# SBUF tiles moved to multiples of 1 or 2 KB, and the low part of q laid on all 128 rows, in a two-block hybrid kernel

## The chip, the cores and the metric

The kernel runs on one core of a Trainium2 chip. The metric is device microseconds of one execution. A core has a matrix engine (TensorE, PE in the profile; its weight loads are shown as PEld), VectorE (DVE), ScalarE (ACT), GpSimd (POOL) and a queue engine (SyncE, SP) that issues the DMAs here. SBUF is the on-chip memory from which TensorE reads: a matmul has a stationary operand, loaded beforehand, and a moving operand that is streamed through; the product is added up in PSUM.

## The reference

512 tokens of width 1024 pass through two blocks. The first has two layers, each with softmax attention (8 heads of 64, relative bias) beside a retention path (4 heads of 128), gated and projected out. The second is a conformer: four gated feed-forward networks of width 2816, one convolution of 31 taps and one stick-breaking attention of 16 heads. The part of the softmax attention that matters here:

```python
scores = jnp.einsum("bnqhd,bnkhd->bnhqk", qc, kb) * (dh ** -0.5)
...
scores = jnp.where(valid, scores + bias[None, None], NEG_INF)
p = jax.nn.softmax(scores, axis=-1)
out = jnp.einsum("bnhqk,bnkhd->bnqhd", p, vb)
```

and the last feed-forward and norm: `h = h + HALF_STEP * swiglu_ffn(...)`, then `rms_norm_2(h, final_norm)`.

## The kernel before, in words

All activations stand transposed: 8 tiles `x` of 128 channels by 512 tokens. Every float32 operand of a large product is split into a rounded high part and the low rest (`split`, `scale_split`, `prepare` and `flush` for the weights), and `mm3` (L252 to L257) makes a product of three matmuls: high by high (L255), high weight by low activation (L256), low weight by high activation (L257). The weights come from HBM in pairs of blocks (`raw`), ACT rounds them (`wh`, L210) and DVE forms the rest (`wl`, L217) one or two blocks ahead of use. The order of the work on each engine is the order in which the program is written.

All large tiles come from one pool, `sb`, under tags: `x`, `raw`, `wh`, `wl`, `u` (32 buffers of 2 KB for each partition), `xg` (16 of 2 KB, the split activations that a projection streams) and `b` (8 of 5 KB, attention matrices and, as high and low halves of one tile, the hidden activations of a feed-forward, L871). In the pool a tag's buffers lie one after the other, behind the tags used before it. The constants lie ahead of the pool, and the small columns (`small`, L128) are a tag of the pool too; the first of them are made after `wl` and before the first `b`. In the built program `x`, `raw`, `u`, `xg`, `wh` and `wl` start 32 bytes past a multiple of 1 KB, and `b` 160 bytes past a multiple of 1 KB.

The softmax attention of a layer (in `hybrid`, L596) goes by four pairs of heads. For a pair `part("w_in", p)` projects q, then k is projected (L729 to L734, with the transposes of the pair before, `flip`, in between), then the gate. `q_out` (L680) scales q and lays out its two heads: `hi` holds the high part of a head on both halves of the 128 rows, `lo` the low part of both heads, each on its own 64 rows. `k_out` (L691) puts a head's high part on its own 64 rows and its low part on the other 64. `scores` (L701) makes, for each of four blocks of 128 queries, two matmuls into one place: L708 over 128 rows (high q by high and low k) and L709 over 64 rows (low q by high k). `softmax1` and `softmax2` follow on DVE and ACT while TensorE projects for the next pair.

Constants that only the set-up and a few later steps read: `cs` (L351, identity, triangle and a stripe of diagonals), `ident` (L357, read by `flip` L570 and `to_rows` L316), the stripe (L954, read by `diagonals` in the convolution).

Of the kernel before, what the change touches and what calls it, by code (L numbers as in the profile page):

```python
# [8 lines left out]
F32 = mybir.dt.float32  # L9
F32R = mybir.dt.float32r  # L10
I32 = mybir.dt.int32
AF = mybir.ActivationFunctionType
ALU = mybir.AluOpType

P = 128
# [17 lines left out]
CLIP = 256  # L33
EPS = 1e-6
LN_EPS = 1e-5
OFF = {512: 0, 384: 512, 128: 896, 256: 1024}


# [56 lines left out]
class Kernel:  # L95
    def __init__(self, ctx, tc, w, x, pos, vec, cst, relb, dec, out):
        self.tc = tc
        self.nc = tc.nc
        self.win, self.xin, self.pos, self.vecin, self.cst, self.relb, self.dec, self.out = (
            w, x, pos, vec, cst, relb, dec, out)  # L100
        self.pc = ctx.enter_context(tc.tile_pool(name="const", bufs=1))
        self.sb = ctx.enter_context(tc.tile_pool(name="sb", bufs=1))
        self.ps = ctx.enter_context(tc.tile_pool(name="ps", bufs=2, space=bass.MemoryType.PSUM))
        self.psb = None
        self.dr = ctx.enter_context(tc.tile_pool(name="dram", bufs=2, space=bass.MemoryType.DRAM))
        self.n = 0
        self.order = weight_order()
        self.chunks = []
        seen = {}
        for i in range(0, len(self.order), 2):  # L110
            k = self.order[i][3]
            assert self.order[i + 1][3] == k
            self.chunks.append((k, seen.get(k, 0)))
            seen[k] = seen.get(k, 0) + 1
        self.loaded = self.ready = self.used = 0
        self.raw = {}
        self.split_w = {}
        self.pending = []
# [8 lines left out]

    def small(self, cols):  # L128
        self.n += 1
        return self.sb.tile([P, cols], F32, name=f"s{self.n}", tag=f"small{cols}", bufs=4)  # L130

    def const(self, shape, dtype=F32):
        self.n += 1
# [210 lines left out]
    def setup(self):  # L344
        nc = self.nc
        nc.scalar.preload_act_table(AF.Sin)
        self.vec = self.const([P, NVEC])
        self.x = [self.tile("x") for _ in range(KT)]
        self.load_pieces()
        self.load()  # L350
        cs = self.const([P, 3, P])  # L351
        nc.sync.dma_start(cs, self.cst)
        nc.sync.dma_start(self.vec[:, 16:NVEC], self.vecin[:, 16:NVEC])
        self.posi = self.tile("u", I32)
        nc.sync.dma_start(self.posi, self.pos.partition_broadcast(P))
        self.cs = cs
        self.ident = cs[:, 0]  # L357
        self.ones2 = self.const([P, 2])
        nc.vector.memset(self.ones2, 1.0)
        self.mean = self.const([P, P])  # L360
        nc.gpsimd.memset(self.mean, 1.0 / D)
        self.mhalf = self.const([P, 4])
        nc.vector.memset(self.mhalf, -0.5)
        self.identr = self.const([P, P], F32R)
        self.tri = self.const([P, P], F32R)
        self.ones = self.const([P, P], F32R)
        self.rest = self.const([P, P], F32R)
        self.nmask = self.const([P, P], F32R)
        self.halfpi = self.const([P, 1])
        nc.vector.memset(self.halfpi, math.pi / 2)  # L370
        self.fgg = self.const([P, KT])
        self.hbias = self.const([P, 16])
        self.acc = None
        self.xg = []
        for m in range(KT):
            self.xg.append(self.scale_split(self.x[m], self.col("norm_gain", m)))
            if m == 2:
                self.acc = self.square_add(self.acc, self.x[0], 0)
            self.prepare_pieces(m)
        for m in range(1, SQ):  # L380
            self.acc = self.square_add(self.acc, self.x[m], m)

    def setup2(self):
        nc = self.nc
        cs = self.cs
        nc.vector.tensor_copy(out=self.identr, in_=cs[:, 0])
        nc.vector.tensor_scalar(self.tri, cs[:, 1], -1.0, 0.0, op0=ALU.mult, op1=ALU.add)
        nc.vector.tensor_scalar(self.ones, cs[:, 1], 0.0, -1.0, op0=ALU.mult, op1=ALU.add)
        nc.vector.tensor_scalar(self.rest, cs[:, 1], 1.0, -1.0, op0=ALU.mult, op1=ALU.add)
        nc.vector.tensor_scalar(self.nmask, cs[:, 1], -1.0e30, 0.0, op0=ALU.mult, op1=ALU.add)  # L390
        fg, g1 = COLS["final_gain"], COLS["ffn1_norm_2"]
        nc.vector.tensor_tensor(out=self.fgg, in0=self.vec[:, fg : fg + KT], in1=self.vec[:, g1 : g1 + KT], op=ALU.mult)
        b = COLS["conv_b_pw1_2"]
        nc.vector.tensor_scalar(self.hbias, self.vec[:, b : b + 16], 0.5, 0.0, op0=ALU.mult, op1=ALU.add)

        pf = self.tile("u")
        nc.vector.tensor_copy(out=pf, in_=self.posi)
        ang = self.tile("u")
        nc.vector.tensor_scalar(ang, pf, self.vec[:, COL_FREQ : COL_FREQ + 1], 0.0, op0=ALU.mult, op1=ALU.add)
        kk = self.tile("u")  # L400
        magic = 12582912.0
        nc.vector.tensor_scalar(kk, ang, 1.0 / (2 * math.pi), magic, op0=ALU.mult, op1=ALU.add)
        nc.vector.tensor_scalar(kk, kk, magic, 0.0, op0=ALU.subtract, op1=ALU.add)
        c1 = 6.28125
        c2 = 0.0019350051879882812
        c3 = 2 * math.pi - c1 - c2
        for c in (c1, c2, c3):
            nc.vector.scalar_tensor_tensor(out=ang, in0=kk, scalar=-c, in1=ang, op0=ALU.mult, op1=ALU.add)
        lim = 3.1415925
        nc.vector.tensor_scalar(ang, ang, lim, -lim, op0=ALU.min, op1=ALU.max)  # L410
        return ang
# [184 lines left out]
    def hybrid(self, l):  # L596
        nc = self.nc
# [4 lines left out]
        q, k = qk[:, 0:S], qk[:, S : 2 * S]  # L602
# [18 lines left out]
        q = self.rotary(q)  # L621
        k = self.rotary(k)
        vs = self.v_pairs_end(v, False)
        q = self.split(q)
        k = self.split(k)
        vs += self.v_pairs("w_in", 26, X, False)
        o, late = None, None
# [7 lines left out]
        for h in range(4):  # L635
            if h > 0:
                q = self.mm()
                self.proj(q, self.take("w_in", 16 + h), X)
                self.ahead(flush=False)
                t = self.ret_weights(d, s)  # L640
                d = self.decay(h)
                q = self.rotary(q)
                k = self.mm()
# [3 lines left out]
                q = self.split(q)  # L647
                o, sq = self.ret_out1(vs[h - 1], t)
                k = self.rotary(k)
# [5 lines left out]
            if h > 0:  # L655
                r = self.ret_out2(sq)
                k = self.split(k)
            self.proj(gp, w, X, 4)
            self.ahead(flush=h == 3)
            s = self.packed_scores(k, q, slice(0, P), True)  # L660
# [5 lines left out]
        o, sq = self.ret_out1(vs[3], vs[4])  # L666
# [5 lines left out]
        def halves(t):  # L672

            hi = self.tile("b", F32R, [P, 2, S])
            for i in range(2):
                r = slice(64 * i, 64 * i + 64)
                nc.scalar.copy(hi[r, i], t[r])
            return hi

        def q_out(ps):  # L680

            t = self.tile("u")
            nc.vector.scalar_tensor_tensor(out=t, in0=ps, scalar=0.125, in1=self.rb, op0=ALU.mult, op1=ALU.mult)
            hi, lo = halves(t), self.tile("u", F32R)
            for i in range(2):
                r, other = slice(64 * i, 64 * i + 64), slice(64 - 64 * i, 128 - 64 * i)
                DUP(nc)(hi[other, i], t[r])
                nc.vector.tensor_tensor(out=lo[r], in0=t[r], in1=hi[r, i].bitcast(F32), op=ALU.subtract)
            return hi, lo

        def k_out(ps):  # L691
# [9 lines left out]
        def scores(q, k, i):  # L701

            o = self.bg()
            r = slice(64 * i, 64 * i + 64)
            for t in (3, 2, 1, 0):
                n = P * (t + 1)
                c, x = slice(OFF[n], OFF[n] + n), slice(P * t, P * t + P)
                nc.tensor.matmul(o[:, c], lhsT=q[0][:, i, x], rhs=k[:, i, 0:n], start=True, stop=False)  # L708
                nc.tensor.matmul(o[:, c], lhsT=q[1][r, x], rhs=k[r, i, 0:n], start=False, stop=True)  # L709
            return o  # L710

        def part(name, c, flush=True):
# [9 lines left out]
        for p in range(4):  # L722
            bias = [self.bias_tile(l, 2 * p), self.bias_tile(l, 2 * p + 1)]
            q = part("w_in", p, False)
# [196 lines left out]
    def conv(self):  # L921
# [3 lines left out]
        nc = self.nc  # L925
# [21 lines left out]
        def diagonals(c):  # L947

            col = COL_DQ + sum(PE_TAPS[:c])
            d = []  # L950
            for j in range(0, PE_TAPS[c], 16):
                n = min(16, PE_TAPS[c] - j)
                t = self.tile("u", F32, [P, 16, 32])
                nc.vector.tensor_tensor(out=t[:, 0:n], in0=self.cs[:, 2:3, 0:32].to_broadcast([P, n, 32]),  # L954
                                        in1=self.vec[:, col + j : col + j + n].unsqueeze(2).to_broadcast([P, n, 32]),
                                        op=ALU.mult)
                d += [t[:, i] for i in range(n)]
            return d
# [631 lines left out]
```

## Time and profile before

| what | value |
|---|---|
| three runs | 2552.58, 2549.5 and 2549.57 us; median 2549.57 |
| the profiled execution | 2552.01 us, its span 2550.2 us |
| TensorE busy | 2516.0 us, 99% of the span |
| VectorE busy | 1347.8 us, 53% |
| ScalarE busy | 894.3 us, 35% |
| GpSimd busy | 173.9 us, 7% |
| mean granted TensorE clock | 0.987 |
| DMA | 92 GB/s in the mean |

A matmul of the page lasts longer than it holds the engine, since the next one starts before it ends: how fast TensorE goes is read from the distance between two starts. "bg<-xg,wh" is a matmul that writes a PSUM tile bg, with a moving operand of the tag xg and a stationary one of the tag wh; "64*128 64x512" means that 64 rows and 128 columns of the array are used and that 512 columns are streamed.

### The profile page before, as it was taken

To read this page: it belongs to the slowest core of one execution; us is meant where nothing else is said; L and a number is where in the kernel's file an instruction comes from. 1 tells how busy PE (TensorE), PEld (TensorE's weight loads), DVE (VectorE), ACT (ScalarE), POOL (GpSimd) and SP (SyncE) were. 2 spreads that over 40 slices of the span, in tenths; PEclk is the share of its full clock that TensorE was granted. 3 is DMA by queue.
4 is the path that set the end of the run, shared out by engine and by line. 5 is a ranking of instruction groups with operands and counts; after the bars stand their busy time and mean duration, and the time that the engine had idled before them with its cause. 6 is when DMAs were issued, how large, how long until landed. Compare 5 with 4: busy or idle time off the path is not lost.

```text
span 2550.2 us, 29339 instructions
## 1 busy us (share of the span) xinstructions
PE 2516.0 (99%) x12124; PEld 2050.9 (80%) x12124; DVE 1347.8 (53%) x1896; ACT 894.3 (35%) x1266; POOL 173.9 (7%) x160
## 2 busy tenths in 40 slices
PE   8999999999999999989999999999999999999998
PEld 7887889778888887668888888888888877888887
DVE  7756565655534446875444443444444786444443
ACT  4334422544222234553222232222223575322222
POOL 2200111002000000330000010000001001000001
PEclk9998999999999999989999999999999999999999
DMA  4231233213222222313222223222222101322221
GB/s 171 89 130 61 83 117 103 87 54 107 91 99 91 99 99 92 99 57 104 91 99 91 99 97 106 83 91 100 92 104 93 50 34 50 103 91 97 104 88 66
DMA packets 49589, 233.76 MB, mean 92 GB/s; under 512 B 12720, under 2 KB 15152, under 8 KB 27568
## 3 DMA queue, kind: packets, MB, share of 16 engines
q1 hardware_dynamic: 49456, 231.88, 26.1%
q8 instruction: 96, 1.57, 0.3%
q14 instruction: 37, 0.30, 0.1%
HBM read 225.67 MB, written 2.13 MB: 89 GB/s over the span
## 4 chain that ended last, share of the span: by engine, by line
PE 91%; DVE 4%; DMA 2%; ACT 2%; issue 1%; POOL 0%; SPq 0%; DVEq 0%; ACTq 0%; POOLq 0%
PE bg L255 14%; PE bg L256 14%; PE bg L257 14%; PE mm L255 12%; PE mm L256 12%; PE mm L257 12%; PE part L1286 1%; PE part L1321 1%; PE mm L588 1%; PE part L255 1%; PE part L256 1%; PE part L257 1%; DMA d<-s 1%; DVE wl L217 1%; PE bg L709 1%
## 5 line engine op out<-in xcount | busy, mean ns | idle before, releaser
L217 DVE TENSOR_TENSOR wl<-raw,wh 128x1024 fp32r<-128x1024 f32 (+1 forms) x406 | 494.4, 1244 | 180.7 <-ACT wh L210 178.4
L255 PE MATMUL bg<-xg,wh 128*128 128x512 f32 x1440 | 563.1, 391 | 7.4 <-ACT wh L194 5.5
L256 PE MATMUL bg<-xg,wh 128*128 128x512 f32 x1440 | 562.3, 391 | 0.0
L257 PE MATMUL bg<-xg,wl 128*128 128x512 f32 x1440 | 562.0, 390 | 0.3 <-DVE wl L195 0.3
L210 ACT CAST wh<-raw 128x1024 fp32r<-128x1024 f32 (+1 forms) x406 | 403.0, 1028 | 412.2 <-PE mm L256 221.9
L255 PEld LDWEIGHTS bg<-xg,wh 128*128 128x128 f32 x1440 | 271.5, 189 | 64.9 <-ACT wh L194 5.9
L257 PEld LDWEIGHTS bg<-xg,wl 128*128 128x128 f32 x1440 | 271.4, 188 | 57.2 <-DVE wl L195 0.7
L256 PEld LDWEIGHTS bg<-xg,wh 128*128 128x128 f32 x1440 | 271.3, 188 | 57.1 <-DVE xg L282 1.1
L255 PE MATMUL mm<-b,wh 128*128 128x512 f32 (+1 forms) x672 | 264.6, 394 | 0.0
L257 PE MATMUL mm<-b,wl 128*128 128x512 f32 (+1 forms) x672 | 264.5, 394 | 0.0
L256 PE MATMUL mm<-b,wh 128*128 128x512 f32 (+1 forms) x672 | 264.5, 394 | 0.0
L867 DVE TENSOR_TENSOR u<-bg,u 128x512 f32<-128x512 f32 x88 | 60.8, 690 | 381.7 <-PE bg L257 361.7
L868 ACT ACTIVATE u<-u 128x512 f32<-128x512 f32 x88 | 55.7, 633 | 561.2 <-DVE u L867 561.2
L296 POOL TENSOR_TENSOR u<-u,u 128x512 f32<-128x512 f32 x61 | 82.6, 1358 | 1843.0 <-ACT u L294 1842.5
L458 DVE SCALAR_TENSOR_TENSOR x<-mm,x 128x512 f32<-128x512 f32 x111 | 76.5, 689 | 223.9 <-PE mm L257 223.8
L255 PE MATMUL mm<-xg,wh 128*128 128x512 f32 x400 | 164.6, 411 | 0.0
L256 PE MATMUL mm<-xg,wh 128*128 128x512 f32 x400 | 159.8, 400 | 0.0
L257 PE MATMUL mm<-xg,wl 128*128 128x512 f32 x400 | 159.8, 399 | 0.0
L257 PEld LDWEIGHTS mm<-b,wl 128*128 128x128 f32 x672 | 126.1, 188 | 30.3
L256 PEld LDWEIGHTS mm<-b,wh 128*128 128x128 f32 x672 | 126.1, 188 | 30.2
L255 PEld LDWEIGHTS mm<-b,wh 128*128 128x128 f32 x672 | 126.2, 188 | 30.1
L255 PE MATMUL mm<-u,wh 128*128 128x512 f32 x248 | 98.6, 398 | 0.6 <-DVE u L1230 0.6
(249 smaller groups left out, 3460.6 us busy)
## 6 DMA issues: line engine op xcount, KB each, us to landing
raw<-w SPq DMA_DIRECT2D x171, 1024.0 KB, 4.8
raw<-w SPq DMA_DIRECT2D x32, 896.0 KB, 4.5
b<-dec SPq DMA_DIRECT2D x8, 640.0 KB, 7.1
u<-relb SPq DMA_DIRECT2D x16, 256.0 KB, 5.2
u<-d SPq DMA_DIRECT2D x14, 256.0 KB, 5.8
b<-b SPq DMA_DIRECT2D x32, 66.0 KB, 2.0
x<-x SPq DMA_DIRECT2D x8, 256.0 KB, 6.1
out<-b SPq DMA_DIRECT2D x8, 256.0 KB, 2.8
```

Source lines behind the costliest of these rows:

```text
L210: nc.scalar.copy(hi[:, s], raw[:, s])
L217: self.nc.vector.tensor_tensor(out=lo[:, s], in0=raw[:, s], in1=hi[:, s].bitcast(F32), op=ALU.subtract)
L255: nc.tensor.matmul(out, lhsT=a[0], rhs=b[0], start=start, stop=False)
L256: nc.tensor.matmul(out, lhsT=a[0], rhs=b[1], start=False, stop=False)
L257: nc.tensor.matmul(out, lhsT=a[1], rhs=b[0], start=False, stop=stop)
L296: eng.tensor_tensor(out=acc, in0=acc, in1=sq, op=ALU.add)
L458: nc.vector.scalar_tensor_tensor(out=x, in0=ps, scalar=scale, in1=x, op0=ALU.mult, op1=ALU.add)
L588: self.nc.tensor.matmul(o[r, P * t : S], lhsT=v[:, t, r], rhs=pt[i][:, OFF[n] : OFF[n] + n], start=t == 0, stop=t == 3)
L709: nc.tensor.matmul(o[:, c], lhsT=q[1][r, x], rhs=k[r, i, 0:n], start=False, stop=True)
L867: nc.vector.tensor_tensor(out=a, in0=o[:, 0:S], in1=self.rb, op=ALU.mult)
L868: nc.scalar.activation(a, a, AF.Silu)
L1286: nc.tensor.matmul(o[:, c : c + n], lhsT=k[i][r, P * t : P * t + P], rhs=q[j][r, P * t : S], start=(i, j) == (0, 0) and t < 3, stop=i == 1 ...
```

## The change

Two things are changed. First, the places of the large tiles: the small columns go to a pool of their own ahead of `sb`, with a filler of 96 bytes; the constant `cs` of 1.5 KB becomes a passing `u` tile, `ident` becomes the same bytes as `identr`, and a copy of the 32 stripe columns (`stripe`) takes the place of the part of `cs` that the convolution reads. In the built program `x`, `raw`, `u`, `xg`, `wh` and `wl` then start at a multiple of 2 KB and `b` at a multiple of 1 KB. Second, `q_out` writes the low part of each head on both halves of the rows, into two tiles instead of one, and the second matmul of `scores` runs over all 128 rows; it thereby also adds the product of the low parts of q and k.

```diff
+FILLER = 24
...
         self.pc = ctx.enter_context(tc.tile_pool(name="const", bufs=1))
+        self.sm = ctx.enter_context(tc.tile_pool(name="small", bufs=1))
         self.sb = ctx.enter_context(tc.tile_pool(name="sb", bufs=1))
+
+        self.sm.tile([P, FILLER], F32, name="filler")
...
-        return self.sb.tile([P, cols], F32, name=f"s{self.n}", tag=f"small{cols}", bufs=4)
+        return self.sm.tile([P, cols], F32, name=f"s{self.n}", tag=f"small{cols}", bufs=4)
...
-        cs = self.const([P, 3, P])
+        cs = self.tile("u")[:, 0 : 3 * P].rearrange("p (a b) -> p a b", a=3)
...
-        self.ident = cs[:, 0]
...
         self.identr = self.const([P, P], F32R)
+        self.ident = self.identr.bitcast(F32)
+        self.stripe = self.const([P, 32])
...
+        nc.vector.tensor_copy(out=self.stripe, in_=cs[:, 2, 0:32])
...
-            hi, lo = halves(t), self.tile("u", F32R)
+            hi, lo = halves(t), [self.tile("u", F32R), self.tile("u", F32R)]
             for i in range(2):
                 r, other = slice(64 * i, 64 * i + 64), slice(64 - 64 * i, 128 - 64 * i)
                 DUP(nc)(hi[other, i], t[r])
-                nc.vector.tensor_tensor(out=lo[r], in0=t[r], in1=hi[r, i].bitcast(F32), op=ALU.subtract)
+                for rows in (r, other):
+                    nc.vector.tensor_tensor(out=lo[i][rows], in0=t[r], in1=hi[r, i].bitcast(F32), op=ALU.subtract)
             return hi, lo
...
-            r = slice(64 * i, 64 * i + 64)
             for t in (3, 2, 1, 0):
...
-                nc.tensor.matmul(o[:, c], lhsT=q[1][r, x], rhs=k[r, i, 0:n], start=False, stop=True)
+                nc.tensor.matmul(o[:, c], lhsT=q[1][i][:, x], rhs=k[:, i, 0:n], start=False, stop=True)
...
-                nc.vector.tensor_tensor(out=t[:, 0:n], in0=self.cs[:, 2:3, 0:32].to_broadcast([P, n, 32]),
+                nc.vector.tensor_tensor(out=t[:, 0:n], in0=self.stripe.unsqueeze(1).to_broadcast([P, n, 32]),
```

On VectorE, at `q_out` of the first pair of layer 0 (u_1381 or u_1387 is the scaled q, b_1383 or b_1389 its high part), there stood before:

```order
L683 SCALAR_TENSOR_TENSOR u_1381<-mm_1352,u_359 128x512
L687 CAST b_1383<-u_1381 64x512
L688 TENSOR_TENSOR u_1386<-u_1381,b_1383 64x512
L687 CAST b_1383<-u_1381 64x512
L688 TENSOR_TENSOR u_1386<-u_1381,b_1383 64x512
L694 TENSOR_TENSOR u_1416<-mm_1391,u_359 128x512
```

and now:

```order
L689 SCALAR_TENSOR_TENSOR u_1387<-mm_1358,u_365 128x512
L693 CAST b_1389<-u_1387 64x512
L695 TENSOR_TENSOR u_1392<-u_1387,b_1389 64x512
L695 TENSOR_TENSOR u_1392<-u_1387,b_1389 64x512
L693 CAST b_1389<-u_1387 64x512
L695 TENSOR_TENSOR u_1393<-u_1387,b_1389 64x512
L695 TENSOR_TENSOR u_1393<-u_1387,b_1389 64x512
L701 TENSOR_TENSOR u_1425<-mm_1400,u_365 128x512
```

Two subtractions of 64 rows by 512 columns are added to each pair, and stand ahead of the scaling of k; nothing else of the pair moves.

On TensorE, the end of the first head's scores and the start of the second's, in the same pair, before (b_1418 is the split k, b_1383 the high part of q, u_1386 the low part of both heads):

```order
L708 MATMUL bg_1466<-b_1418,b_1383 128x128
L709 MATMUL bg_1466<-b_1418,u_1386 128x128
L708 MATMUL bg_1475<-b_1418,b_1383 128x512
L709 MATMUL bg_1475<-b_1418,u_1386 128x512
L708 MATMUL bg_1475<-b_1418,b_1383 128x384
L709 MATMUL bg_1475<-b_1418,u_1386 128x384
```

and now:

```order
L714 MATMUL bg_1475<-b_1427,b_1389 128x128
L715 MATMUL bg_1475<-b_1427,u_1392 128x128
L714 MATMUL bg_1484<-b_1427,b_1389 128x512
L715 MATMUL bg_1484<-b_1427,u_1393 128x512
L714 MATMUL bg_1484<-b_1427,b_1389 128x384
L715 MATMUL bg_1484<-b_1427,u_1393 128x384
```

The order is the same, and so is the number of matmuls and of columns; the low part of q now comes from a tile for each head, u_1392 and u_1393, and is used over 128 rows. The rest of TensorE's order does not change.

## Rows read from the trace of the kernel before

**Rows 1.** The page: busy time of TensorE, its granted clock in tenths in 40 slices, and the chain that ended last, by engine.

```profile
PE 2516.0 (99%) x12124; PEld 2050.9 (80%) x12124; DVE 1347.8 (53%) x1896; ACT 894.3 (35%) x1266; POOL 173.9 (7%) x160
...
PEclk9998999999999999989999999999999999999999
...
PE 91%; DVE 4%; DMA 2%; ACT 2%; issue 1%; POOL 0%; SPq 0%; DVEq 0%; ACTq 0%; POOLq 0%
```

**Rows 2.** The longest of TensorE's waits, over the whole span: who waited for whom, us in total, times, longest.

```profile
PE mm L1003 <- DVE u L954: 8.2, 1, 8.2
```

**Rows 3.** The timeline of TensorE at the scores of one head of the last pair of layer 0, in order: start us, duration us, engine, line, operation; the ninth row is the start of the second head's.

```profile
247.52 0.50 PE L708 MATMUL bg<-b,b 128*128 128x512 f32 x1
247.95 0.50 PE L709 MATMUL bg<-b,u 64*128 64x512 f32 x1
248.38 0.44 PE L708 MATMUL bg<-b,b 128*128 128x384 f32 x1
248.75 0.43 PE L709 MATMUL bg<-b,u 64*128 64x384 f32 x1
249.12 0.38 PE L708 MATMUL bg<-b,b 128*128 128x256 f32 x1
249.43 0.38 PE L709 MATMUL bg<-b,u 64*128 64x256 f32 x1
249.75 0.33 PE L708 MATMUL bg<-b,b 128*128 128x128 f32 x1
250.00 0.32 PE L709 MATMUL bg<-b,u 64*128 64x128 f32 x1
250.26 0.51 PE L708 MATMUL bg<-b,b 128*128 128x512 f32 x1
```

**Rows 4.** The timeline of TensorE in a feed-forward's gate and up projections, moving tiles of the tag xg: the first of 45 matmuls that follow one another without another between them, and the last.

```profile
1299.81 0.39 PE L255 MATMUL bg<-xg,wh 128*128 128x512 f32 x1
...
1309.78 0.39 PE L257 MATMUL bg<-xg,wl 128*128 128x512 f32 x1
```

**Rows 5.** The timeline of TensorE: in a projection of v, two matmuls of 256 columns with six between them; and the ten transposes of 128 columns of one `flip`, as one row.

```profile
134.19 0.28 PE L255 MATMUL bg<-wh,xg 128*128 128x256 f32 x1
...
135.03 0.28 PE L256 MATMUL bg<-wl,xg 128*128 128x256 f32 x1
...
204.37 1.25 PE L570 MATMUL bg<-c,b 128*128 128x128 f32 x10
```

**Rows 6.** One source line's instructions over the span: engine, operation, tiles, count; duration ns least, median, most; first and last start us; forms.

```profile
L708 PE MATMUL bg<-b,b x64: 326/442/688, 161.9 to 543.0; 128*128 128x512 f32 x16, 128*128 128x384 f32 x16, 128*128 128x256 f32 x16, 128*128 128x128 f32 x16
```

**Rows 7.** Stretches of the softmax attention of both layers: us from and to, their length, busy time and count of PE, PEld, DVE, ACT and POOL, the granted clock (1.00 is 2.4 GHz, 0.50 is 1.2 GHz), DMA share, GB/s.

```profile
191.90:198.60 6.70, 6.70 (x16) 4.53 (x15) 4.53 (x23) 3.69 (x13) 0.29 (x2) 0.50 0.00 0
...
222.60:229.30 6.70, 6.70 (x16) 5.08 (x17) 4.33 (x19) 5.51 (x17) 0.00 (x0) 0.50 0.00 0
...
253.30:256.60 3.30, 3.30 (x9) 2.58 (x8) 3.16 (x14) 2.90 (x12) 0.00 (x0) 0.50 0.00 0
...
454.70:461.40 6.70, 6.70 (x16) 4.80 (x16) 5.60 (x24) 4.34 (x15) 0.29 (x2) 0.50 0.13 50
...
485.40:488.70 3.30, 3.30 (x9) 2.49 (x10) 2.47 (x12) 2.70 (x9) 0.00 (x0) 0.50 0.00 0
...
512.70:519.40 6.70, 6.70 (x16) 4.94 (x16) 4.09 (x21) 4.93 (x17) 0.00 (x0) 0.50 0.00 0
...
543.50:546.80 3.30, 3.30 (x9) 2.65 (x9) 3.05 (x14) 2.92 (x11) 0.00 (x0) 0.50 0.00 0
```

**Rows 8.** The timeline of TensorE at the second pair of layer 0: the start of the second head's scores, the first matmul behind them, and the fourth, seventh and tenth.

```profile
191.07 0.51 PE L708 MATMUL bg<-b,b 128*128 128x512 f32 x1
...
195.02 0.79 PE L255 MATMUL mm<-xg,wh 128*128 128x512 f32 x1
...
196.47 0.63 PE L255 MATMUL mm<-xg,wh 128*128 128x512 f32 x1
...
197.75 0.63 PE L255 MATMUL mm<-xg,wh 128*128 128x512 f32 x1
...
198.88 0.40 PE L255 MATMUL mm<-xg,wh 128*128 128x512 f32 x1
```

**Rows 9.** Groups of matmuls of one form over the span: line, engine, operation, tiles, form, count, busy us, mean ns of one, idle us before them. Each stands for three groups of about that count, of the lines L255 to L257.

```profile
L255 PE MATMUL bg<-xg,wh 128*128 128x512 f32 x1440 | 563.1, 391 | 7.4 <-ACT wh L194 5.5 <-ACT u L868 1.9
...
L257 PE MATMUL mm<-b,wl 128*128 128x512 f32 x664 | 262.3, 395 | 0.0
...
L255 PE MATMUL mm<-xg,wh 128*128 128x512 f32 x400 | 164.6, 411 | 0.0
...
L255 PE MATMUL mm<-u,wh 128*128 128x512 f32 x248 | 98.6, 398 | 0.6 <-DVE u L1230 0.6
...
L255 PE MATMUL part<-xg,wh 128*128 128x512 f32 x144 | 57.1, 397 | 0.0
```

**Rows 10.** The timeline of TensorE in a feed-forward's down projection, moving tiles of the tag b: two matmuls with thirteen between them.

```profile
699.70 0.39 PE L257 MATMUL mm<-b,wl 128*128 128x512 f32 x1
...
702.96 0.39 PE L256 MATMUL mm<-b,wh 128*128 128x512 f32 x1
```

**Rows 11.** VectorE: the subtraction of `q_out`, all of them, in the columns of rows 6; and the scaling of k in the second pair of layer 0, from the timeline, with the idle time before it and what ended that.

```profile
L688 DVE TENSOR_TENSOR u<-u,b x16: 682/686/691, 152.6 to 525.2; 64x512 fp32r<-64x512 f32 x16
...
210.22 0.69 DVE L694 TENSOR_TENSOR u<-mm,u 128x512 f32<-128x512 f32 x1 [4.47 <-PE mm L257]
```

## The prediction

> **What bounds the kernel now.** I read the page first. TensorE is busy for 2516.0 us, 99% of the span, and holds 91% of the chain that ended last [rows 1]. Its waits come next: the longest is 8.2 us, once, in the convolution [rows 2]. So what counts is not what TensorE waits for but how many starts it makes and how far apart they are. A busy TensorE is not one at its peak, so I read the distance between starts in the timeline, for each shape and tag.
>
> Three things are to be seen. With moving tiles of the tag xg, 44 steps take 1309.78 - 1299.81 = 9.97 us: 0.2266 us for 512 columns [rows 4]. With moving tiles of the tag b, 14 steps of the same shape take 702.96 - 699.70 = 3.26 us: 0.2329 us [rows 10]. And the scores, which alternate between 128 and 64 rows, need 0.43 us for 512 columns, 0.37 for 384, 0.31 for 256 and 0.25 for 128 [rows 3]. That is some 0.2 us over a matmul of such a length elsewhere, on nearly every one, whichever way the number of rows goes. Last, the granted clock: in seven stretches, each starting inside the scores or as they end, it stands at 0.50, that is 1.2 GHz [rows 7]; before each of them TensorE had been making scores at these wide distances. Nine matmuls behind the second pair's scores then take 198.88 - 195.02 = 3.86 us, where 9 x 0.2266 = 2.04 would do [rows 8].
>
> **The change, part by part.** *Scores on 128 rows.* One head's scores take 250.26 - 247.52 = 2.74 us [rows 3]. After the change all eight matmuls have 128 rows. At distances of matmuls that follow others of the same number of rows they take 0.227 for 512 columns [rows 4], 0.12 for 256 (0.84 us for seven steps, [rows 5]), 0.174 for 384 by interpolation, and for 128 about 0.11 (ten in 1.25 us with the last one's full length, [rows 5]): twice their sum is 2 x 0.631 = 1.26 us. There are 64/4 = 16 such heads [rows 6]: 16 x (2.74 - 1.26) = 23.7 us less, all on TensorE. Bounds: nothing, if the distance is due to something other than the change of rows; 2.74 x 16 = 43.8 us cannot be passed. The nearest row is the same three-matmul pattern without the change of rows, so I take 23.7.
>
> *The clock.* From 191.07 to 195.02 the second head of that pair takes 3.95 us instead of 2.74, and the nine matmuls behind it lose 1.82: 3.03 us in a stretch of 6.7 us at half clock, 0.45 us for each us [rows 7, 8]. The seven stretches sum to 36.7 us, which makes 16.6 us. When the scores take 2.5 us for a pair instead of 5.5 and are as dense as a projection, what preceded each fall is gone, so I take all of it. Bounds: nothing, or (if the faster kernel lets the clock fall elsewhere) a few us the other way.
>
> *Places of the tiles, tag b.* Between [rows 4] and [rows 10] shape, rows and stationary tag are the same; what differs is the moving tile, which starts 32 bytes past a multiple of 1 KB for xg and 160 past for b. After the change both start at such a multiple, so b should go at xg's distance: 3 x 664 matmuls [rows 9] x (0.2329 - 0.2266) = 12.5 us less. Bound from the other side: no gain, if the 6 ns have another reason.
>
> *Places of the tiles, all other tags.* No moving tile of the trace starts at a multiple of 1 KB, so the price of this has to be bounded. Below: at 1.2 GHz three matmuls take 197.75 - 196.47 = 1.28 us, 0.427 us each, which is 512 columns at one a cycle with nothing over [rows 8]; at 2.4 GHz the same would be 0.2133, and xg's 0.2266 is 13 ns above that. These 13 ns could depend on the address as b's 19 ns do. They concern 3 x (1440 + 400 + 248 + 144) = 6696 matmuls [rows 9]: 89 us, and for b another 26. Above: the distance could grow as well as shrink, since the stationary tiles now start at the same multiples as the moving ones. I take the nearest row, 32 bytes away: no change for these, 0 us.
>
> *VectorE.* Two more subtractions for each of 8 pairs: 16 x 0.686 = 11.0 us [rows 11]. They stand between q's arrival and the scaling of k, before which VectorE now idles 4.47 us for TensorE's projection of k [rows 11]; 2 x 0.686 = 1.4 us of that goes, and with TensorE some 3 us quicker at the scores VectorE reaches `q_out` that much later relative to it. What queues behind them is the scaling of k, the weights' low parts and the gate; TensorE needs k only after the gate's 24 matmuls, 5.4 us later. Cost 0; if that cover were gone, 11.0 us. The copy of the stripe is one small copy in set-up, and `cs` in a `u` tile is read only there: 0.
>
> Sum, against the profiled execution: 2552.0 - 23.7 - 16.6 - 12.5 = 2499.2 us. The median of the runs shown is 2.4 us below that execution, so I forecast 2497 us.
>
> **The rivals.**
>
> *Aligned tiles reach the floor.* If the distance above 0.2133 us is the price of tiles that start off such a multiple, all streams fall to it, and the time is 2497 - 89 - 26 = 2382 us; half way it is about 2440. For it: b and xg show that the start of a tile moves the distance at all, and at half clock, where the stream asks for half as many bytes in a ns, the surplus is gone [rows 8], as for a memory that cannot quite feed the stream. Against it: the 256-column matmuls, which read two separate runs, also lose about 13 ns (0.12 against 0.107), no more than the 512-column ones that read one run twice as long as either [rows 4, 5]; a cost of every matmul, whatever it reads, would look like that. The Trainium skill (TensorE: Matmul & The Clock Gate, section Back-to-back issue gap) gives N/2.4 + 2.5 ns for isolated warm matmuls, 215.8 ns at 512 columns; by that as the reachable distance the estimate would be near 2403 us. The trace shows no stream as quick as that.
>
> *Only the rows change.* The surplus of b has nothing to do with its start, and the clock still falls in or behind each pair's softmax stage. Then 2552.0 - 23.7 - 2.4 = 2526 us. For it: the transposes and the two-headed value products, which stay, are also short matmuls next to the scores. Against it: each fall begins inside the scores or right behind them [rows 3, 7], none at the transposes [rows 5], and b and xg differ in nothing else that the rows show.
>
> *The streams collide.* Moving and stationary tiles start at the same multiples, and a stream and the weight load beside it get in each other's way. If the distance grew to as far above b's as b's is above xg's, 0.2392 us, the cost would be 6696 x 12.6 ns + 1992 x 6.3 ns = 97 us against b and xg today; with the 40.3 us of scores and clock that is 2552.0 - 40.3 + 97 - 2.4 = 2606 us. It decides from a common distance of 0.2327 us on, about b's today: there the kernel is no faster than before. For it: alignment has changed the distance already, in a direction that no row explains. Against it: xg and the weights already start at the same offset from a multiple of 512 bytes, 32, and that is the quicker case. The Trainium skill (SBUF — State Buffer, section Who interferes with whom) gives TensorE two read ports of its own, for the moving operand and for the weights; by that this rival falls out, but so would b's surplus, which the trace shows.
>
> *VectorE becomes the bound* in the attention stage: 2497 + 11 = 2508 us, which lies in the forecast's own range.
>
> **How the numbers follow.** The forecast, with its VectorE variant, has 0.44 and a range of its own from 2480 to 2515 us. The floor or a part of the way to it has 0.36, between 2380 and 2475. Only the rows: 0.13. Collision: 0.07, of which 0.05 ends slower and 0.02 near the time of before. A change below 0.2%, 5 us, cannot be told from none here. Faster is therefore 0.44 + 0.36 + 0.13 = 0.93, the same 0.02, slower 0.05. For 8 in 10 the range must take in most of the floor's case and most of the rows' case: 2380 to 2530 us.
>
> **What would show it.** Scores: one head in about 1.26 us with steps of 0.227, 0.174, 0.12 and 0.11 us. Clock: no stretch at 0.50 between 190 and 550 us of the span. Tiles: the distance in a down projection equal to that in a gate projection; if both lie under 0.222 us, the floor's rival is right, if both lie over 0.2327, the collision. VectorE: idle time before the scaling of k still above zero, and no wait of TensorE for `q_out` or `softmax2`. The forecast is wrong if the distance of the xg stream moves, and wrong in the scores if matmuls of 128 rows keep the 0.2 us between them.

## The result and the profile after

| what | before | after |
|---|---|---|
| median of four runs each | 2550.92 us | 2495.45 us |
| lowest and highest | 2549.5, 2552.58 | 2493.22, 2496.6 |
| profiled execution, its span | 2552.01, 2550.2 | 2495.15, 2492.9 |
| mean granted TensorE clock | 0.987 | 0.995 |

The changed kernel takes 0.9781 of the time of before, with a 95% interval from 0.9764 to 0.9798. The forecast was 2497 us. The page of the profile after, its busy times and its chain as in [rows 1]:

```profile
PE 2460.9 (99%) x12124; PEld 2033.2 (82%) x12124; DVE 1357.4 (54%) x1913; ACT 892.9 (36%) x1266; POOL 173.9 (7%) x160
...
PE 90%; DVE 4%; DMA 3%; ACT 2%; issue 1%; POOL 0%; SPq 0%; DVEq 0%; ACTq 0%; POOLq 0%
```

TensorE issues the same 12,124 matmuls and is still 99% busy, but its busy time is 55 us shorter, nearly the whole difference of the spans. The share says nothing of that; the distances between starts do. The timeline of TensorE after the change, at the same scores as [rows 3], with the matmul that follows the second head:

```profile
232.48 0.50 PE L714 MATMUL bg<-b,b 128*128 128x512 f32 x1
232.81 0.40 PE L715 MATMUL bg<-b,u 128*128 128x512 f32 x1
233.05 0.33 PE L714 MATMUL bg<-b,b 128*128 128x384 f32 x1
233.22 0.34 PE L715 MATMUL bg<-b,u 128*128 128x384 f32 x1
233.40 0.28 PE L714 MATMUL bg<-b,b 128*128 128x256 f32 x1
233.52 0.28 PE L715 MATMUL bg<-b,u 128*128 128x256 f32 x1
233.64 0.22 PE L714 MATMUL bg<-b,b 128*128 128x128 f32 x1
233.69 0.28 PE L715 MATMUL bg<-b,u 128*128 128x128 f32 x1
233.81 0.44 PE L714 MATMUL bg<-b,b 128*128 128x512 f32 x1
...
235.07 0.45 PE L259 MATMUL mm<-u,wh 128*128 128x512 f32 x1
```

One head now takes 1.33 us (233.81 - 232.48) and the other 1.26 (235.07 - 233.81), where [rows 3] had 2.74. The first head's steps behind its first are 0.24, 0.17, 0.18, 0.12, 0.12, 0.05 and 0.12 us; its first step of 0.33 follows a value product, which stands there in the kernel before too.

Two streams of the same timeline, the gate and up projections of a feed-forward (46 steps) and a down projection (47 steps), which answer to [rows 4] and [rows 10]:

```profile
1259.79 0.39 PE L261 MATMUL bg<-xg,wl 128*128 128x512 f32 x1
...
1270.21 0.39 PE L259 MATMUL bg<-xg,wh 128*128 128x512 f32 x1
...
647.26 0.39 PE L259 MATMUL mm<-b,wh 128*128 128x512 f32 x1
...
657.91 0.39 PE L261 MATMUL mm<-b,wl 128*128 128x512 f32 x1
```

The tag xg takes 10.42 / 46 = 0.2265 us a step, as in before; the tag b 10.65 / 47 = 0.2266 us instead of 0.2329. The softmax attention of the two layers by stretches, after, in the columns of [rows 7]:

```profile
150.00:260.00 110.00, 110.00 (x565) 88.58 (x564) 81.31 (x187) 58.91 (x115) 1.88 (x9) 1.00 0.26 89
...
420.00:520.00 100.00, 100.00 (x521) 80.31 (x520) 76.58 (x181) 54.10 (x109) 1.16 (x8) 1.00 0.26 87
```

The granted clock is 1.00 through all of it. Of VectorE, the source lines of the subtraction in `q_out` and of the scaling of k, the second with the idle time before it (what ended that, us, times), after and, last, before:

```profile
L695 DVE TENSOR_TENSOR u<-u,b x32: 682/686/691, 152.3 to 494.7; 64x512 fp32r<-64x512 f32 x32
```

```profile
L701 DVE TENSOR_TENSOR u<-mm,u x8: 691/692/692, 156.3 to 495.4; 128x512 f32<-128x512 f32 x8
...
  PE mm L261: 1.7, 2
...
  PE mm L257: 29.2, 8
```

The sixteen added subtractions are there, at 0.686 us each. VectorE now waits for the projection of k in two pairs out of eight, 1.7 us in all, where it waited in all eight, for 29.2 us.

Adding up the distances between all neighbouring starts on TensorE in both traces gives this account; the sum is 56.5 us. The first row takes all 128 score matmuls of before at the mean distance that their form has at full clock, and what they and others took beyond that in the seven stretches stands in the second.

| where | us less |
|---|---|
| the scores of the 16 heads, all counted at full clock (43.6 to 20.5 us) | 23.1 |
| what the half clock of the seven stretches added, to scores and other matmuls | 16.7 |
| down projections, moving tiles of the tag b | 13.8 |
| everything else, most of it between 600 and 620 us and at one wait of a gate projection, 1184 us into the span of before | 2.9 |

### The profile page after: what moved, and what is told of

Read it like the earlier page. It is cut to its first block, busy times and chain, and to the rows that moved or that the text cites. A ratio compares the mean times of both kernels' runs of the same rounds, so it can differ in the third digit from the quotient of the medians.

```text
span 2492.9 us, 29349 instructions
## 1 busy us (share of the span) xinstructions
PE 2460.9 (99%) x12124; PEld 2033.2 (82%) x12124; DVE 1357.4 (54%) x1913; ACT 892.9 (36%) x1266; POOL 173.9 (7%) x160
## 3 DMA queue, kind: packets, MB, share of 16 engines
q8 instruction: 96, 1.57, 0.3%
## 4 chain that ended last, share of the span: by engine, by line
PE 90%; DVE 4%; DMA 3%; ACT 2%; issue 1%; POOL 0%; SPq 0%; DVEq 0%; ACTq 0%; POOLq 0%
PE bg L259 14%; PE bg L260 14%; PE bg L261 14%; PE mm L259 12%; PE mm L260 12%; PE mm L261 12%; DMA d<-s 2%; PE part L1292 1%; PE part L1327 1%; PE mm L594 1%; DVE wl L221 1%; PE part L259 1%; PE part L260 1%; PE part L261 1%; DVE u L1022 1%
## 5 line engine op out<-in xcount | busy, mean ns | idle before, releaser
L259 PE MATMUL mm<-b,wh 128*128 128x512 f32 (+1 forms) x672 | 260.6, 388 | 0.0
L260 PE MATMUL mm<-b,wh 128*128 128x512 f32 (+1 forms) x672 | 260.6, 388 | 0.0
L259 PE MATMUL mm<-xg,wh 128*128 128x512 f32 x400 | 159.5, 399 | 0.0
L260 PE MATMUL mm<-xg,wh 128*128 128x512 f32 x400 | 156.2, 390 | 0.0
```

Of the source, the lines that this page charges most:

```text
L259: nc.tensor.matmul(out, lhsT=a[0], rhs=b[0], start=start, stop=False)
L260: nc.tensor.matmul(out, lhsT=a[0], rhs=b[1], start=False, stop=False)
```

## The experiments

The kernel before took 2559 to 2561 us in the runs beside these experiments, so each is told by its ratio to that, and differences of a few us by runs made together or by the distances in the trace.

**The change in halves.** The first kernel is the one of before with only the low part of q on both halves (with it the product of the low parts is added):

```diff
-            hi, lo = halves(t), self.tile("u", F32R)
+            hi, lo = halves(t), [self.tile("u", F32R), self.tile("u", F32R)]
...
-                nc.tensor.matmul(o[:, c], lhsT=q[1][r, x], rhs=k[r, i, 0:n], start=False, stop=True)
+                nc.tensor.matmul(o[:, c], lhsT=q[1][i][:, x], rhs=k[:, i, 0:n], start=False, stop=True)
```

> The tiles stay where they were before; only the low part of q is laid on all 128 rows. Theory (the scores lost 23.7 us to the change between 128 and 64 rows, and the clock falls followed from that, 16.6 us): 2550 - 40 = 2510 us, one head's scores in 1.26 us, no stretch at half clock between 190 and 550 us, and the down projection's matmuls (moving tag b) still at 0.233 us. Rival (the clock falls have another cause, such as the transposes or the value products near the scores): 2526 us, with the seven stretches at half clock still there.

It took 2516.11 us (2511.42 to 2517.92) against 2559.07: 0.9821, interval 0.9795 to 0.9846. Its stretches of the attention, and a group of its down projections:

```profile
150.00:260.00 110.00, 110.00 (x566) 88.60 (x565) 81.54 (x188) 59.29 (x116) 2.29 (x9) 1.00 0.26 89
...
420.00:520.00 100.00, 100.00 (x521) 80.36 (x521) 76.25 (x181) 54.01 (x108) 1.17 (x8) 1.00 0.25 87
```

```profile
L257 PE MATMUL mm<-b,wl 128*128 128x512 f32 x664 | 262.3, 395 | 0.0
```

The rows alone bring the clock to 1.00, and the matmuls of the tag b keep the 395 ns of [rows 9].

The second is the changed kernel with only the low part of q as it was:

```diff
-            hi, lo = halves(t), [self.tile("u", F32R), self.tile("u", F32R)]
+            hi, lo = halves(t), self.tile("u", F32R)
...
-                nc.tensor.matmul(o[:, c], lhsT=q[1][i][:, x], rhs=k[:, i, 0:n], start=False, stop=True)
+                nc.tensor.matmul(o[:, c], lhsT=q[1][r, x], rhs=k[r, i, 0:n], start=False, stop=True)
```

> The tiles at multiples of 1 or 2 KB, the scores with 64 rows for the low part as before. Theory (only the matmuls that stream a tile of the tag b gain, 1992 of them by 6.3 ns): 2550 - 12.5 = 2537 us, the seven stretches at half clock between 190 and 550 us still there, one head's scores still in 2.74 us. Rival (the places also have a part in the clock falls or in the scores): well below 2530 us, with fewer stretches at half clock.

It took 2546.14 us (2539.42 to 2547.57): 0.9939, interval 0.9915 to 0.9962. Two of its stretches and the same group:

```profile
165.90:172.50 6.60, 6.60 (x15) 4.57 (x15) 5.64 (x24) 4.05 (x14) 0.29 (x2) 0.50 0.16 61
...
196.60:203.20 6.60, 6.60 (x17) 5.11 (x17) 4.54 (x19) 5.49 (x17) 0.00 (x0) 0.50 0.00 0
```

```profile
L261 PE MATMUL mm<-b,wl 128*128 128x512 f32 x664 | 258.3, 389 | 0.0
```

Seven stretches at half clock are still there between 160 and 550 us, and b is quick. So the clock belongs to the rows and b's distance to the places. The two halves save 43.0 and 12.9 us, 55.9 together, against the whole change's 55.5. The intervals leave some 6 us either way on each half; within that they add up.

**Own start or relative start.** The forecast said that b was slow because its own tiles began 160 bytes past a multiple of 1 KB. Another reading of [rows 4, 10] is that b began elsewhere than the weights, and xg at the same place as they. In the first of two kernels, both made from the changed one, all tiles start 128 bytes past such a multiple:

```diff
-FILLER = 24
+FILLER = 24 + 32
```

> The changed kernel with every large tile 128 bytes further on, so that all start 128 bytes past a multiple of 1 KB. Theory R (the distance of two matmuls depends on where the moving tile starts relative to the stationary one): all streams stay at 0.2266 us, 2495 us. Theory A (it depends on where the moving tile itself starts): xg, u and b all go at 0.233 us, 8688 matmuls by 6.3 ns, 2495 + 55 = 2550 us.

In the second a gap ahead of the first `wh` tile moves the weights and b by 128 bytes, and xg and u stay at a multiple:

```diff
+            self.sb.tile([P, 32], F32, name="gap")
```

> The changed kernel with 128 bytes put ahead of wh, so that the split weights wh and wl and the tag b start 128 bytes past a multiple of 1 KB, and x, raw, u and xg at such a multiple. Theory R (relative start): b beside the weights at 0.2266 us, but the streams of xg and u, 6696 matmuls, at 0.233 us or more, 2495 + 42 = 2537 us. Theory A (the moving tile's own start): xg and u at 0.2266 us, b at 0.233 us, 2495 + 12.5 = 2508 us.

They took 2504.81 us (0.979) and 2533.54 us (0.990), one run each. The timeline of the second kernel, 55 steps of a gate and up projection and 15 of the down projection behind it:

```profile
639.21 0.39 PE L262 MATMUL bg<-xg,wl 128*128 128x512 f32 x1
...
651.99 0.40 PE L260 MATMUL bg<-xg,wh 128*128 128x512 f32 x1
...
656.17 0.40 PE L260 MATMUL mm<-b,wh 128*128 128x512 f32 x1
...
659.58 0.39 PE L260 MATMUL mm<-b,wh 128*128 128x512 f32 x1
```

xg, whose own start has not moved, now takes 12.78 / 55 = 0.2324 us a step, and b, which left its multiple, 3.41 / 15 = 0.2273. With everything at 128 all are quick. What counts for these matmuls is where the moving tile starts relative to the stationary one. Over the whole trace the steps of xg and u grew by 39.6 us against the changed kernel and those of b by 0.4; the spans differ by 2531.4 - 2492.9 = 38.5 us.

**How fine.** The same with gaps of 64, 256 and 32 bytes ahead of the weights and as many more ahead of b, so that the weights lie one gap past xg and b one gap past the weights. The edit with 64 bytes (16 columns; 64 and 8 in the other two):

```diff
+            self.sb.tile([P, 16], F32, name="gap")
...
+        if not self.gapped:
+            self.gapped = True
+            self.sb.tile([P, 16], F32, name="gap2")
```

> The changed kernel with 64 bytes put ahead of wh and 64 more ahead of b: the weights start 64 bytes behind the multiple at which xg and u start, and b 64 bytes behind the weights'. Theory (two streams that read from TensorE's side meet at fixed places; the start relative to each other counts, zero is the quickest): xg and u above 0.2266 us, b above 0.2266 us, the time above 2495 us by as many us as 8.7 for each ns. Rival (any common multiple of 64 bytes is as good as zero, and 128 was a bad place only for b and xg by chance of the 128): both stay at 0.2266 us, 2495 us. A distance below 0.2266 us for one of the two signs would be a gain that neither kernel has.

> The changed kernel with 256 bytes put ahead of wh and 256 more ahead of b. Theory (relative start counts, with a period of 512 bytes at most, since the 512-byte steps from one weight block to the next change nothing): some distance for xg, u and b alike, because 256 ahead and 256 behind are the same place in such a period; above 0.2266 us if zero is the quickest place. Rival (only 128 is bad, the period is 256): 0.2266 us for all, 2495 us.

> The changed kernel with 32 bytes put ahead of wh and 32 more ahead of b. Theory (relative start counts, by the byte): a distance other than 0.2266 us for xg, u or b. Rival (the step that counts is 64 bytes or more): 0.2266 us for all, 2495 us.

They took 2540.44 us (0.992), 2501.37 (0.977) and 2546.08 (0.994), one run each, against one run of the kernel before, 2561.06. Groups of the kernel with 256 bytes, and of that with 32:

```profile
L263 PE MATMUL bg<-xg,wl 128*128 128x512 f32 x1440 | 561.9, 390 | 0.3 <-DVE wl L201 0.3
...
L261 PE MATMUL mm<-b,wh 128*128 128x512 f32 x664 | 258.3, 389 | 0.0
```

```profile
L263 PE MATMUL bg<-xg,wl 128*128 128x512 f32 x1440 | 570.5, 396 | 0.3 <-DVE wl L201 0.3
...
L263 PE MATMUL mm<-b,wl 128*128 128x512 f32 x664 | 262.3, 395 | 0.0
```

All seven kernels together, with the mean distance of neighbouring 512-column matmuls on the high weights, half-clock steps and waits left out:

| kernel | weights, xg, b start past a multiple of 1 KB, bytes | xg, us | b, us |
|---|---|---|---|
| before | 32, 32, 160 | 0.2270 | 0.2333 |
| after | 0, 0, 0 | 0.2270 | 0.2267 |
| all at 128 | 128, 128, 128 | 0.2271 | 0.2268 |
| weights and b at 128 | 128, 0, 128 | 0.2330 | 0.2269 |
| gaps of 64 | 64, 0, 128 | 0.2334 | 0.2280 |
| gaps of 256 | 256, 0, 512 | 0.2270 | 0.2267 |
| gaps of 32 | 32, 0, 64 | 0.2333 | 0.2333 |

Every pair of tiles whose starts differ by nothing or by a multiple of 256 bytes is at 0.2267 to 0.2271 us; every pair that differs by 32 or 128 is at 0.2330 to 0.2333; 64 depends on the sign (0.2334 where the moving tile starts 64 bytes below the weights, 0.2280 where it starts 64 above, 0.2308 for the latter on the low weights).

**What the 64 rows cost.** The changed kernel with 64-row low parts, but a head's four matmuls of 128 rows first and its four of 64 rows behind them: two changes of the number of rows for each head instead of eight, and the same columns.

```diff
...
-                nc.tensor.matmul(o[:, c], lhsT=q[0][:, i, x], rhs=k[:, i, 0:n], start=True, stop=False)
-                nc.tensor.matmul(o[:, c], lhsT=q[1][i][:, x], rhs=k[:, i, 0:n], start=False, stop=True)
+                nc.tensor.matmul(o[:, c], lhsT=q[0][:, i, x], rhs=k[:, i, 0:n], start=t > 0, stop=False,
+                                 skip_group_check=True)
+            for t in (3, 2, 1, 0):
+                n = P * (t + 1)
+                c, x = slice(OFF[n], OFF[n] + n), slice(P * t, P * t + P)
+                nc.tensor.matmul(o[:, c], lhsT=q[1][r, x], rhs=k[r, i, 0:n], start=False, stop=True,
+                                 skip_group_check=True)
```

> The tiles at multiples of 1 or 2 KB as in the changed kernel, the low part of q on 64 rows as before, but a head's four matmuls of 128 rows first and its four of 64 rows behind them, so that the number of rows changes twice for a head instead of eight times. Theory (each change of the number of rows costs about 0.2 us, whatever stands on either side): one head's scores in 1.26 + 2 x 0.2 = 1.66 us, 6.4 us over the 16 heads behind the changed kernel without a fall of the clock, 2502 us, and up to 2515 us with some falls. Rival (a matmul of 64 rows is itself the slow one): some 0.2 us on each of the four 64-row matmuls, 2.1 us for a head, 13 us or more behind the changed kernel.

It took 2509.8 us (0.980), one run. Its timeline at the last pair of layer 0, four score matmuls to a row, with the matmul that follows the second head:

```profile
234.61 0.86 PE L714 MATMUL bg<-b,b 128*128 128x512 f32 x4
235.40 0.85 PE L719 MATMUL bg<-b,u 64*128 64x512 f32 x4
236.18 0.84 PE L714 MATMUL bg<-b,b 128*128 128x512 f32 x4
236.95 0.85 PE L719 MATMUL bg<-b,u 64*128 64x512 f32 x4
237.73 0.50 PE L259 MATMUL mm<-u,wh 128*128 128x512 f32 x1
```

The pair's two heads take 1.57 and 1.55 us, 237.73 - 234.61 = 3.12 together, where they take 1.33 and 1.26, 235.07 - 232.48 = 2.59 together, with 128 rows throughout: 0.53 more for four changes, so some 0.13 for each. That is less than the 0.40 a head that was expected, and 8 x 0.53 = 4.2 us of the distance to the changed kernel, which by the ratios (0.980 against 0.9776, below) is about 6. A group of four takes 0.77 to 0.79 us whichever its rows are: matmuls of 64 rows are not slow, the change is. No stretch at half clock is left between 190 and 550 us, though half of these matmuls have 64 rows. The clock's fall came with the wide distances, not with the 64 rows.

**Further in the same direction.** The stick-breaking attention has the same pattern: per head twelve matmuls of 64 rows (L1292) and, in two places between and behind them, mask matmuls of 128 rows (L1296). Three kernels ran together. The first is the changed kernel again.

> The changed kernel again, on the chip of the two that follow, to compare them with: 0.978 of the kernel before.

It took 2502.85 us (2500.25 to 2504.7) against 2561.07: 0.9776, interval 0.9751 to 0.9801, the ratio of the first measurement. The second puts a head's four masks first, so that two changes of rows remain instead of four.

```diff
-        def scores(h, ts):
+        def scores(h):
...
+            for t in (1, 2, 3, 0):
+                o, c = (z[h, 1], 0) if t == 0 else (z[h, 3], OFF[S - P * t] - S)
+                nc.tensor.matmul(o[:, c : c + P], lhsT=self.identr, rhs=self.nmask, start=t < 3, stop=False,
+                                 skip_group_check=True)
...
-            for t in ts:
-                c = 0 if t == 0 else OFF[S - P * t] - S
-                nc.tensor.matmul(o[:, c : c + P], lhsT=self.identr, rhs=self.nmask, start=False, stop=True,
-                                 skip_group_check=True)
```

> The changed kernel; in the stick-breaking attention a head's four mask matmuls of 128 rows come first and its twelve score matmuls of 64 rows behind them, so that the number of rows changes twice for a head instead of four times. Theory (a change of rows costs 0.1 to 0.2 us wherever it stands): 16 heads x 2 x 0.15 = 5 us less than the changed kernel. Rival (there the change of rows is hidden behind the weight loads of the short mask matmuls): no change.

It took 2497.93 us (2495.02 to 2498.66): 0.9753, interval 0.9733 to 0.9773. The intervals of the ratios overlap, but all four of its runs lie below all four of the changed kernel's. One head in the changed kernel's timeline, and one in this kernel's, the latter with the idle time before all mask matmuls (what ended it, us, times):

```profile
2000.95 1.43 PE L1292 MATMUL part<-u,u 64*128 64x384 f32 x9
2002.31 0.55 PE L1296 MATMUL part<-c,c 128*128 128x128 f32 x3
2002.79 0.96 PE L1292 MATMUL part<-u,u 64*128 64x512 f32 x3
2003.68 0.33 PE L1296 MATMUL part<-c,c 128*128 128x128 f32 x1
2003.85 0.44 PE L259 MATMUL mm<-xg,wh 128*128 128x512 f32 x1
```

```profile
2004.96 0.56 PE L1288 MATMUL part<-c,c 128*128 128x128 f32 x4
2005.44 2.16 PE L1296 MATMUL part<-u,u 64*128 64x384 f32 x12
2007.54 0.50 PE L259 MATMUL mm<-xg,wh 128*128 128x512 f32 x1
...
  ACT b L1334: 2.1, 5
```

Where nothing waits a head takes 2.58 us instead of 2.90: 0.16 us for each change of rows left out. For 16 heads that would be 5.1 us, near the 4.9 between the medians, but the profiled execution does not give that much in this stage. The masks, now first, wait for ScalarE five times, 2.1 us in all, and behind one of these waits the granted clock is 0.50 from 1974.3 to 1977.7 us, where it is 1.00 in the changed kernel; from the matmul ahead of the first head to the one behind the last the stage is 2.1 us shorter (123.7 against 125.8). By its ratio this kernel is the quickest of those that ran.

The third lays q and k of that attention out on 128 rows as the softmax scores have them, two products instead of three, with the copies and subtractions on VectorE.

```diff
-            qs[p] = self.split(q, eng=nc.vector)
+            hi, lo = [[self.tile("u", F32R) for _ in range(2)] for _ in range(2)]
...
+                for rows in (r, other):
+                    nc.vector.tensor_copy(out=hi[i][rows], in_=q[r])
+                for rows in (r, other):
+                    nc.vector.tensor_tensor(out=lo[i][rows], in0=q[r], in1=hi[i][r].bitcast(F32), op=ALU.subtract)
...
+                for j in range(2):
+                    nc.tensor.matmul(o[:, c : c + n], lhsT=k[:, P * t : P * t + P], rhs=q[j][h % 2][:, P * t : S],
+                                     start=False, stop=j == 1, skip_group_check=True)
```

> The changed kernel; in the stick-breaking attention q and k are laid out as in the softmax attention, so that a head's scores are two products over 128 rows for each block instead of three over 64, with the masks first. Theory: no change of rows is left there, and a third of 1280 x 3 columns is gone: 16 x (4 x 0.15 + 1280 x 0.443 ns = 0.57) = 19 us less than the changed kernel, with 35 us more of VectorE in a stage in which it idles 40% of the time. Rival (VectorE, which makes q's and k's parts just ahead of a pair's scores, becomes late): TensorE waits for it at each pair, and the gain is eaten up.

It took 2517.65 us (2515.95 to 2518.46): 0.9831, interval 0.9812 to 0.9851, 15 us behind the changed kernel. Its timeline where nothing waits, the waits of its TensorE (us, times, longest), and the whole stage, with one stretch in it, in the columns of [rows 7]:

```profile
2020.03 0.56 PE L1300 MATMUL part<-c,c 128*128 128x128 f32 x4
2020.42 1.48 PE L1307 MATMUL part<-u,u 128*128 128x384 f32 x8
2021.74 0.40 PE L259 MATMUL mm<-xg,wh 128*128 128x512 f32 x1
```

```profile
PE part L1338 <- DVE b L1326: 11.1, 8, 5.8
...
PE mm L259 <- DVE u L1272: 5.3, 3, 4.5
...
PE part L1307 <- DVE u L1290: 4.2, 3, 1.8
```

```profile
1930.00:2080.00 150.00, 130.73 (x686) 104.72 (x684) 136.34 (x225) 90.74 (x131) 2.42 (x2) 0.92 0.10 36
1964.60:1971.40 6.80, 4.31 (x15) 3.96 (x16) 6.58 (x12) 1.61 (x4) 0.00 (x0) 0.50 0.19 80
```

TensorE gets its gain: a head takes 2021.74 - 2020.03 = 1.71 us instead of 2.90, 19 us over 16 heads. But VectorE's busy time over the span rises by 35 us, from 1357.6 in the changed kernel beside it to 1392.7, and in these 150 us of the stage it is busy for 136.3, against 116.9 in the changed kernel, where it thus idled 22% of the time and not the 40% that was expected. TensorE waits 20.6 us for it in those three rows, and the clock, which is 1.00 in this stage of the changed kernel, is 0.92 here, some 24 us at half clock; the stretch shown begins within a wait, the 4.5 us of the second row. The stage as a whole is 13.7 us longer than in the changed kernel, so beside 19 us gained and 20.6 waited some 12 us are left for the clock, an estimate by subtraction. A quicker TensorE and a fuller VectorE spend the same margin twice.

## Why the forecast held, point by point

*Bound.* Right: the number of starts and the distances between them set the time, and the busy share showed nothing of either.

*Scores on 128 rows.* Right in mechanism and size: 23.7 us forecast, 23.1 measured at full clock. The mark set for it, one head in about 1.26 us, is in the timeline. That it is met so closely is in part luck: the two matmuls of 128 columns take 0.17 us together where the sum had 0.22, and the first head's first step 0.33 where it had 0.227. That the number of rows is the cause, and not the 64-row matmul as such, the grouped kernel shows: it kept the 64 rows, and all but 0.27 us of the 1.44 a head (23.1 / 16) was gone.

*The clock.* Right: 16.6 us forecast, 16.7 measured; no stretch at half clock between 190 and 550 us. The halves tie it to the rows (gone in the one, there in the other), the grouped kernel to the wide distances.

*Places, tag b.* The gain is right, 12.5 us forecast against 13.8, but the reason given for it is not. The step "After the change both start at such a multiple, so b should go at xg's distance" takes a tile's own start for the cause. The row with all tiles 128 bytes off a multiple is as quick as the changed kernel, and xg at a multiple becomes slow when the weights leave it. The text had the right rule in hand and used it only against a rival: xg and the weights had the same offset, and that was the quicker case. The term came out by luck, since the change happens to give b both. The size was low because b's mean distance over the span is 0.2333 us, not the 0.2329 of the fourteen steps read, and since, by the account of the distances, 696 rather than 664 matmuls of each line gain.

*Places, other tags.* Right: xg's distance did not move (0.2265 after, 0.2266 before). For this no reason was known, only the nearest row; the runs supply it, since xg, u and the weights shared their start before as well.

*VectorE.* Right at 0 us, but with little to spare. Of the 29.2 us of idle time before the scaling of k 1.7 is left, and the sign "still above zero" holds in two pairs of eight. The prediction's own numbers said as much, since 4.47 less 1.4 less some 3 us leaves next to nothing. TensorE did not come to wait for `q_out` or `softmax2`, and the last experiment shows what a further 35 us on VectorE do in a like place.

*The rivals.* The floor (0.36) did not come, and no placement tried brought a stream under 0.226 us; at least 13 ns over the 0.2133 stayed at each, which is what the argument against this rival, from the 512 and the 256 columns, would lead one to expect. "Only the rows change" is wrong in both its parts: b's surplus went with the places alone, and with the rows alone, at 0.9821 instead of 0.9781, the clock no longer fell. The collision has its sign turned round: equal starts are quick, and xg goes at 0.233 us in a kernel that pulls it and the weights apart, where the rival gave 0.2392 to aligned ones. By the Trainium skill (SBUF — State Buffer, section Who interferes with whom) two read ports of its own would leave nothing for such a start to act on; the trace disagrees, with 0.2324 against 0.2265 us on the same stream. By what means the start acts no run shows.

## What to carry to other kernels

Read the distance between starts for each tag and shape, not the busy share: a stream that is some per cent wider than its twin, or short matmuls 0.2 us further apart than others of their length, are gains that 99% busy hides, and the wide distances may cost the clock as well. Keep the number of rows the same from one matmul to the next, by laying the data out or, where the engine that would do this has no time, by grouping the matmuls of equal rows. And before a difference in address is put down to a tile's own place, move the other operand too.

## What the runs showed that was not expected

- The start of the moving tile relative to the stationary one moves the distance of 512-column matmuls by 6 ns, 0.227 to 0.233 us, with a period of 256 bytes among the gaps tried; 64 bytes cost all of it in one direction and less in the other.
- For the 256-column matmuls of the projection of v it goes the other way, in small: with the weights 32 bytes past xg, 36 steps take 138.10 - 133.87 = 4.23 us, 0.1175 each, where they take 0.12 at equal starts [rows 5]. Why is open. The timeline of the kernel with gaps of 32:

```profile
133.87 0.28 PE L263 MATMUL bg<-wh,xg 128*128 128x256 f32 x1
...
138.10 0.28 PE L263 MATMUL bg<-wh,xg 128*128 128x256 f32 x1
```

- The 13 ns that 0.2266 us lies above 512 columns at 2.4 GHz stayed at every placement tried. What they are was not found.
- A change between 128 and 64 rows costs some 0.13 to 0.16 us where matmuls of equal rows are grouped and 0.18 where every matmul changes ((2.74 - 1.33) / 8), and in the softmax attention the granted clock fell with the latter alone.
